# First convolution tap on ScalarE, and the first weights in another layout and queue

## The chip, the cores and the metric

The kernel runs on one core of a Trainium2 chip. The metric is device time in microseconds (us), the median of several executions. The core's engines work side by side, each through its own list of instructions in a fixed order, with semaphores between them: TensorE (PE: matmuls, weight loads shown as PEld), VectorE (DVE), ScalarE (ACT), GpSimd (POOL) and SyncE (SP, which here only issues DMAs). DMAs are issued from SP, ACT or POOL.

## The reference

One layer of a streaming encoder, on x of 1024 rows (the sequence) by 1024 columns, float32:

```python
h = x @ w_in + b_in                     # -> [xa | za | xb | zb | ga | gb], 1024 columns each
xa = causal_depthwise_conv(xa, conv_w, conv_b)          # 4 taps along the sequence
ya = rg_lru(xa, w_r, b_r, w_i, b_i, lam) * silu(za)     # branch A: gates, then a linear scan
yb = multiscale_pool(xb, w_pool, b_pool, scale) * silu(zb)   # branch B: windows 2, 4, 8, 16
merged = sigmoid(ga) * (ya @ w_proj_a) + sigmoid(gb) * (yb @ w_proj_b)
y = merged @ w_out + b_out
out = layer_norm(alpha * x + y, ln_gain, ln_bias)
```

The convolution of branch A is `y[t] = sum over k = 0..3 of x[t - 3 + k] * w[k], plus b`, per channel.

## The kernel before

All matmuls are in a split form: every float32 operand is split into a high part (a copy into the rounded type `F32R`, by ACT: `A.copy`) and a low part (raw minus high, by DVE), and a product is three passes: high x high, high x low, low x high (`passes`). On top of that the big products are done in blocks of halves with Strassen's scheme: seven products where eight would be, from sums of operands. The steps named m1 to m7 in class `Group` are these seven.

The feature axis is cut into blocks of 128 columns of h. A group takes two such blocks: `G` groups make gate columns (ga or gb), `A` groups the pair xa, za, and `B` groups the pair xb, zb. The list `order` runs G0, then A0, G1, A1, G2 and so on, then the B groups. After the groups come the two projections (`pa`, `pb`), and the product with `w_out` with the norm and the stores.

The first group, G0, has a path of its own, because nothing has been loaded yet: it is done without the seven products, as four quarters of x (`q`) times halves of the contraction (`kh`) and of the sequence (`h`), for both of its blocks (`n` = 0 and 1, blocks 32 and 36 of `w_in`). Its matmuls are called `ps_s` in the profile. Their weights lie in `wr[n]` (raw, `w0r` in the profile), `wh[n]` (high, `w0h`) and `wl[n]` (low, `w0l`). `dma_w0(n, a, b, h)` loads the parts a to b (of four, 128 rows of the contraction each) of block n, for one or both halves `h`; `split_w0` splits them. `dma_x(q, i, sl)` loads a piece of `xr[q][i]`, which holds two halves of x's quarter q; `split_x` splits it into `x13` (kh = h), `x2` and `xb` in the profile `x` and `xb`. For quarter 0 this goes piece by piece, in this order:

```python
    split_w0(0, 0, 1, slice(0, 1))
    for kh, h in ((0, 0), (1, 1), (0, 1), (1, 0)):
        if kh == h == 1:
            split_w0(0, 0, 1, slice(1, 2))
        for sl in PARTS if kh == h == 0 else (slice(0, H),):
            split_x(0, kh, h, sl)
            mm0(0, kh, h, 0, sl)
        if kh == h == 1:
            split_w0(1, 0, 1)
            mm0(0, 0, 0, 1)
        if kh or h:
            mm0(0, kh, h, 1)
```

So PE begins with the first block (n = 0) on two pieces of 256 columns of the half (0, 0), goes on with the first block on the half (1, 1), then the second block (n = 1) on (0, 0), the second block on (1, 1), and both blocks on (0, 1) (tile `xb`) and (1, 0) (tile `x`). `sum57` (the 128x1024 subtraction `t<-xr,xr` on DVE) prepares the sums of x for the groups that follow.

The order on each engine is not the order of the code. Every operation is recorded in a class `Plan`, which keeps PE's order as written and sorts the operations of the others by due times that follow from PE's order, on a clock of estimated costs (`cost`); `emit` then issues them in that order. All instructions therefore have one line number in the profile (L388, in `emit`). `within(us)` sets how long before or after its place in the code an operation is due: `within(-2 * SOON)` is four microseconds ahead, and puts DMAs early in their queue. The planner's costs know a DVE `tensor_scalar` into `xc` and an ACT `activation` with Identity as different prices, so that a moved operation can change the order of others.

`a_front(c, xp, zt)` is the convolution of an A group: from `xp` (the block's xa with three zero columns ahead) it makes `xc` by four taps over 128x1024, then splits `xc` into `xch` and `xcl`; `a_gates` multiplies those with the gate weights (matmuls `ps_g`), and goes on with sigmoid, exp, tanh, sqrt on ACT and the scan on DVE. There are eight A groups.

Of the kernel before, what the change touches and what calls it, by code (L numbers as in the profile page):

```python
# [11 lines left out]
F32 = mybir.dt.float32  # L12
F32R = mybir.dt.float32r
AF = mybir.ActivationFunctionType
ALU = mybir.AluOpType

P = 128
S = 1024
D = 1024
NK = D // P  # L20
# [24 lines left out]
C_CONVB = 48  # L45
C_CONVW = 56
# [354 lines left out]
def layer_kernel(ctx: ExitStack, tc: tile.TileContext, xq, x, w_in, par, wg, w_pool, wpa, wpb, w_out, rows, out):  # L401
    nc = Plan(tc)
# [18 lines left out]
    def wt(name, dt=F32R, shape=(P, 2, H)):  # L421
        return wpool.tile(list(shape), dt, tag="w", name=name)
# [4 lines left out]
    def kt(name, dt=F32, w=S):  # L427
        return kpool.tile([P, w], dt, tag="k", name=name)

    def et(name):  # L430
        return epool.tile([P, H], F32, tag="e", name=name)
# [9 lines left out]
    V, A = nc.vector, nc.scalar  # L441
# [4 lines left out]
    def pcol(base, c):  # L446
        return par_sb[:, base + c:base + c + 1]


    def split(raw, hi, lo):  # L450
        A.copy(hi, raw)
        V.tensor_tensor(lo, raw, hi.bitcast(F32), ALU.subtract)
# [147 lines left out]
    def blocks_of(kind, c):  # L600
        if kind == "A":
            return XA + c, ZA + c
        if kind == "B":
            return XB + c, ZB + c
        sec = GA if c < 4 else GB
        return sec + c % 4, sec + c % 4 + 4
# [141 lines left out]

    def a_front(c, xp, zt):
        xc = kt(f"xc{c}")  # L750
        V.tensor_scalar(xc, xp[:, 0:S], pcol(C_CONVW, 4 * c), pcol(C_CONVB, c), ALU.mult, ALU.add)
        for j in range(1, 4):
            V.scalar_tensor_tensor(xc, xp[:, j:j + S], pcol(C_CONVW, 4 * c + j), xc, ALU.mult, ALU.add)
        xh, xl = kt(f"xch{c}", F32R), kt(f"xcl{c}", F32R)
        split(xc, xh, xl)
        A.activation(zt, zt, AF.Silu, bias=pcol(C_BIN + ZA, c), scale=-1.0)
        return xc, xh, xl
# [146 lines left out]
    def b_pool(g):  # L904
# [15 lines left out]
        if g == 1:  # L920
# [5 lines left out]
    sp, m, nl, y, z, z2, acc = (const.tile([P, 8], F32, name=n)  # L926
                                for n in ("sp", "sp_m", "sp_nl", "sp_y", "sp_z", "sp_z2", "sp_acc"))
# [29 lines left out]
    for i in range(WARM):  # L957
        nc.tensor.matmul(psw, warm[:, 0:P], warm, start=True, stop=True)
    first = blocks_of(*order[0])
    wr, wh, wl = [[f(f"{t}{n}") for n in range(2)] for t, f in  # L960
                  (("w0r", lambda n: wt(n, F32)), ("w0h", wt), ("w0l", wt))]
# [6 lines left out]
    def w0_part(t, n, a, b):  # L968
        return t[n].rearrange("p h (k m) -> p h k m", m=P)[:, :, a:b, :]

    def dma_w0(n, a, b, h=slice(0, 2)):

        (A if a == 0 else nc.sync).dma_start(w0_part(wr, n, a, b)[:, h], w_in[first[n]].rearrange("p (h k) m -> p h k m", h=2)[:, h, a:b, :])

    def split_w0(n, a, b, h=slice(0, 2)):
        split(*(w0_part(t, n, a, b)[:, h] for t in (wr, wh, wl)))

    def dma_x(q, i, sl=slice(0, S)):
        nc.sync.dma_start(xr[q][i][:, sl], xq[q, i][:, sl])
# [21 lines left out]

    PARTS = [slice(0, H // 2), slice(H // 2, H)]
    dma_w0(0, 0, 1, slice(0, 1))
    with nc.within(-2 * SOON):
        for sl in PARTS:
            dma_x(0, 0, sl)
    dma_w0(0, 0, 1, slice(1, 2))
    dma_w0(1, 0, 1)
    dma_x(0, 0, HALF[1])
    dma_x(0, 1, HALF[0])  # L1010
    dma_x(0, 1, HALF[1])
# [65 lines left out]
    def each(f, qs, *a):  # L1077
        for q in qs:
            f(q, *a)

    split_w0(0, 0, 1, slice(0, 1))
    for kh, h in ((0, 0), (1, 1), (0, 1), (1, 0)):
        if kh == h == 1:
            split_w0(0, 0, 1, slice(1, 2))
# [8 lines that stand above are left out]
# [74 lines left out]
    for i in range(1, len(order)):  # L1167
        kind, c = order[i]
# [54 lines left out]
        if kind == "A":  # L1223
            def prev_end(c=c, tiles=tiles, i=i):
                front = a_front(c, *tiles)
                due.setdefault(i + 2, []).append(lambda: a_gates(c, *front, tiles[1]))
        elif kind == "B":
            def prev_end(c=c, tiles=tiles, i=i):
                for _ in b_front(c, *tiles):
                    pass  # L1230
                if c % 2 == 1:
                    pools.setdefault(i + 2, []).append(lambda: b_pool(c // 2))
        else:
            prev_end = finish
# [122 lines left out]
    for i, (n, j) in enumerate(steps):  # L1357
# [7 lines left out]
        if j == 1:  # L1365
            a, c, m1, um = [[None] * KQ for _ in range(4)]
        X_, W_ = ([(hi_[:, k, :], lo_[:, k, :]) for hi_, lo_ in ops[i][o:o + 2] for k in range(2)] for o in (0, 2))
        for g in range(KQ):
# [17 lines left out]
            if (n, j) in DONE:  # L1386
                d, h = DONE[n, j]
                d += g
                if j == 3:
                    t, u = ps, et(f"c12_{n}{g}") if n == "b" else None  # L1390
                else:
                    t = u = m1[g] if j == 2 else um[g][:, HALF[h]]
# [12 lines left out]
            if (n, j, g) in CASTS:  # L1405
                k = CASTS.index((n, j, g))
# [89 lines left out]
    a, c = ([None] * KQ for _ in range(2))  # L1496
# [89 lines left out]
```

## Time and profile before

| what | before |
|---|---|
| median of 3 runs | 742.84 us (742.25, 742.84, 745.42) |
| profiled execution, its own time | 743.09 us |
| its span | 741.3 us |
| PE busy, share of the span | 732.1 us, 99% |
| DVE busy | 599.6 us, 81% |
| ACT busy | 459.0 us, 62% |
| POOL busy | 68.2 us, 9% |
| moved by DMA | 158.98 MB, mean 214 GB/s |

The span runs from the first to the last instruction in the trace; the execution's own time has some 1.8 us around it. A row of a timeline or of the chain gives start, duration, engine, operation, written tile, read tiles, and in brackets how long the engine had stood idle ahead of it and for what. A row of waits gives the waiting instruction, whom it waited for, the sum, the number of times and the longest. A row of windows gives the stretch, its length, and each engine's busy time in it with the number of instructions (PE, PEld, DVE, ACT, POOL), then the granted clock, the DMA share and GB/s. A row of a tile gives durations in ns as least, median and largest.

### The profile page before, as it was taken

The numbers are of one execution on the slowest core, as the hardware profiler recorded it, in microseconds if no ns is written. First come the engines' busy times: TensorE is split into PE (matmuls) and PEld (weight loads), VectorE is DVE, ScalarE is ACT, GpSimd is POOL, SyncE is SP. The second block draws the span as 40 slices with busy tenths as digits, with TensorE's granted clock in tenths as the row PEclk, the third lists the DMA queues.
The fourth block names the chain that finished last, engine by engine and source line by source line (L and its number), as shares of the span: only waits on it lengthen the run. The fifth ranks groups of instructions, "written<-read, shape, count | busy, mean of one in ns | idle before, by whom it ended". The sixth has DMA issues, their size and how long they took to land.

```text
span 741.3 us, 8792 instructions
## 1 busy us (share of the span) xinstructions
PE 732.1 (99%) x3249; PEld 599.0 (81%) x3249; DVE 599.6 (81%) x749; ACT 459.0 (62%) x587; POOL 68.2 (9%) x118
## 2 busy tenths in 40 slices
PE   8999999999999999999999999999999999999996
PEld 6887887888788878888888888888888888888885
DVE  7999796959696878977986767879948886999676
ACT  7686959686877868688844445446543555324473
POOL 0071011111101111100011000100000000000021
PEclk9999999999999999999999999999999999999999
DMA  8237988588988989842187944998679996758657
GB/s 328 96 137 194 273 190 259 139 243 217 307 166 214 321 214 281 213 115 99 45 200 155 213 113 157 277 336 319 229 248 298 317 330 230 261 206 233 179 88 139
DMA packets 64227, 158.98 MB, mean 214 GB/s; under 512 B 4340, under 2 KB 8308, under 8 KB 64120
## 3 DMA queue, kind: packets, MB, share of 16 engines
q1 hardware_dynamic: 43512, 106.26, 41.3%
q0 software_dynamic: 20112, 51.91, 33.6%
q8 instruction: 25, 0.41, 0.2%
q10 hardware_dynamic: 560, 0.26, 0.1%
q14 instruction: 18, 0.15, 0.1%
HBM read 137.43 MB, written 77.07 MB: 289 GB/s over the span
## 4 chain that ended last, share of the span: by engine, by line
PE 98%; DMA 1%; DVE 1%; DVEq 0%; issue 0%
PE a_A L388 11%; PE a_B L388 11%; PE a_G L388 11%; PE oa L388 6%; PE pa_a L388 6%; PE pa_b L388 6%; PE c_B L388 6%; PE c_A L388 6%; PE c_G L388 5%; PE ps_pool L388 3%; PE oc L388 3%; PE pc_b L388 3%; PE pc_a L388 3%; PE e_B L388 3%; PE e_A L388 3%; PE ps_s L388 3%
## 5 line engine op out<-in xcount | busy, mean ns | idle before, releaser
L388 ACT ACT_TABLE_LOAD x38 | 48.8, 1283 | 3.0 <-issue 2.3
L388 DVE TENSOR_TENSOR i<-i,xc 128x1024 f32<-128x1024 f32 x8 | 9.8, 1224 | 26.6 <-ACT i L388 26.6
L388 DVE SCALAR_TENSOR_TENSOR xc<-xp,par_sb,xc 128x1024 f32<-128x1024 f32 x24 | 30.7, 1279 | 0.3
L388 PE MATMUL pa_a<-oh,oh 128*128 128x512 f32 x64 | 24.9, 389 | 0.0
L388 PE MATMUL pa_a<-oh,ol 128*128 128x512 f32 x64 | 24.9, 389 | 0.0
L388 PE MATMUL pa_b<-oh,oh 128*128 128x512 f32 x64 | 24.9, 389 | 0.0
L388 PE MATMUL pa_b<-ol,oh 128*128 128x512 f32 x64 | 24.9, 389 | 0.0
L388 PE MATMUL pa_b<-oh,ol 128*128 128x512 f32 x64 | 24.9, 389 | 0.0
L388 PE MATMUL pa_a<-ol,oh 128*128 128x512 f32 x64 | 24.9, 389 | 0.0
L388 ACT ACTIVATE zb<-zb,par_sb 128x1024 f32<-128x1024 f32 (+1 forms) x16 | 15.0, 939 | 13.7 <-DVE zb L388 13.6
L388 ACT ACTIVATE r<-ps_g,par_sb 64x512 f32<-64x512 f32 x32 | 21.9, 684 | 2.1 <-PE ps_g L388 1.2
L388 ACT ACTIVATE i<-ps_g,par_sb 64x512 f32<-64x512 f32 x32 | 21.9, 685 | 1.9 <-DVE r L388 1.4
L388 PE MATMUL c_A<-x64h,wd_A 128*128 128x512 f32 x64 | 21.0, 389 | 0.0
L388 PE MATMUL c_B<-x64h,wd_B 128*128 128x512 f32 x64 | 21.0, 389 | 0.0
L388 PE MATMUL ps_pool<-mixh,wp 128*128 128x512 f32 x64 | 20.6, 393 | 0.0
L388 POOL DMA_DIRECT2D out<-y x7 | 8.5, 1210 | 132.1 <-ACT sd L388 118.7
L388 PE MATMUL e_A<-x,wah_A 128*128 128x512 f32 x64 | 19.7, 389 | 0.0
L388 PE MATMUL e_B<-x,wah_B 128*128 128x512 f32 x64 | 19.7, 389 | 0.0
L388 POOL COPY paced<-pace 128x1 f32<-128x1 f32 x17 | 6.6, 387 | 128.7 <-ACT pace L388 128.7
L388 PE MATMUL c_G<-x64h,wd_G 128*128 128x512 f32 x56 | 18.4, 389 | 0.0
L388 DVE TENSOR_TENSOR_SCAN r<-a,i 128x1024 f32<-128x1024 f32 x8 | 18.3, 2282 | 0.1
L388 PE MATMUL e_G<-x,wah_G 128*128 128x512 f32 x56 | 17.2, 389 | 0.0
(521 smaller groups left out, 2535.9 us busy)
## 6 DMA issues: line engine op xcount, KB each, us to landing
sg<-sg SPq DMA_DIRECT2D x16, 512.0 KB, 3.6
ra_A<-in_w_in SPq DMA_DIRECT2D x8, 512.0 KB, 7.2
rb_A<-in_w_in SPq DMA_DIRECT2D x8, 512.0 KB, 7.8
xb<-bias SPq DMA_DIRECT2D x4, 1024.0 KB, 15.9
ya<-r SPq DMA_DIRECT2D x8, 512.0 KB, 6.3
xb<-in_x POOLq DMA_DIRECT2D x4, 1024.0 KB, 9.3
ra_B<-in_w_in SPq DMA_DIRECT2D x8, 512.0 KB, 4.8
rb_B<-in_w_in SPq DMA_DIRECT2D x8, 512.0 KB, 6.2
```

Source lines behind the costliest of these rows:

```text
L388: getattr(getattr(nc, t.op[0]), t.op[1])(*a, **k)
```

## The change

Three things are changed.

- In `a_front` the first tap, `xp[:, 0:S] * w[0] + b`, is an ACT activation (Identity with a scale and a bias per partition) instead of a DVE `tensor_scalar`. The three other taps stay on DVE.
- The first group's two weight blocks are laid out in DRAM quarter by quarter (first index the quarter, then the half), so that a quarter of both halves is one contiguous run per partition; the raw tile in SBUF has the same layout, and `split_w0` reads it through `w0_raw`. The high and low tiles keep their layout. The layout is made on the host before the launch.
- The second block's first quarter is issued from SP's queue instead of ACT's. It and the second piece of the first block's first quarter now stand inside `within(-2 * SOON)`. The very first high part (128x128) is made by DVE instead of ACT.

```diff
     def a_front(c, xp, zt):
         xc = kt(f"xc{c}")
-        V.tensor_scalar(xc, xp[:, 0:S], pcol(C_CONVW, 4 * c), pcol(C_CONVB, c), ALU.mult, ALU.add)
+        A.activation(xc, xp[:, 0:S], AF.Identity, bias=pcol(C_CONVB, c), scale=pcol(C_CONVW, 4 * c))
...
+    def w0_raw(n, a, b):
+        t = wr[n].rearrange("p a b -> p (a b)").rearrange("p (k h m) -> p h k m", h=2, m=P)
+        return t[:, :, a:b, :]
+
     def dma_w0(n, a, b, h=slice(0, 2)):
-        (A if a == 0 else nc.sync).dma_start(w0_part(wr, n, a, b)[:, h], w_in[first[n]].rearrange("p (h k) m -> p h k m", h=2)[:, h, a:b, :])
-
-    def split_w0(n, a, b, h=slice(0, 2)):
-        split(*(w0_part(t, n, a, b)[:, h] for t in (wr, wh, wl)))
+        lo_, hi_ = 2 * P * a + P * h.start, 2 * P * (b - 1) + P * h.stop
+        (A if n == a == 0 else nc.sync).dma_start(wr[n].rearrange("p a b -> p (a b)")[:, lo_:hi_],
+                                                  w_in[first[n]].rearrange("p k m -> p (k m)")[:, lo_:hi_])
+
+    def split_w0(n, a, b, h=slice(0, 2), high=A.copy):
+        raw, u, v = w0_raw(n, a, b)[:, h], w0_part(wh, n, a, b)[:, h], w0_part(wl, n, a, b)[:, h]
+        high(u, raw)
+        V.tensor_tensor(v, raw, u.bitcast(F32), ALU.subtract)
...
     with nc.within(-2 * SOON):
         for sl in PARTS:
             dma_x(0, 0, sl)
-    dma_w0(0, 0, 1, slice(1, 2))
-    dma_w0(1, 0, 1)
+        dma_w0(0, 0, 1, slice(1, 2))
+        dma_w0(1, 0, 1)
     dma_x(0, 0, HALF[1])
...
-    split_w0(0, 0, 1, slice(0, 1))
+    split_w0(0, 0, 1, slice(0, 1), V.tensor_copy)
...
+    w0 = blocks(w_in[0])
+    for n in (32, 36):
+        w0[n] = w0[n].reshape(P, 2, 4, P).transpose(0, 2, 1, 3).reshape(P, NK, P)
...
-        "w_in": blocks(w_in[0]),
+        "w_in": w0,
```

## The prediction

> **What bounds the kernel now.** I read the page first: the span, the busy shares, and the chain of work that ended last. Then the waits of TensorE (PE), and the windows.
>
> ```profile
> span 741.3 us, 8792 instructions
> PE 732.1 (99%) x3249; PEld 599.0 (81%) x3249; DVE 599.6 (81%) x749; ACT 459.0 (62%) x587; POOL 68.2 (9%) x118
> PE 98%; DMA 1%; DVE 1%; DVEq 0%; issue 0%
> PE ps_warm L388 <- DVE xp L388: 1.4, 1, 1.4
> PE ps_s L388 <- DVE xb L388: 0.3, 1, 0.3
> 9.95:731.12 721.17, 721.17 (x3205) 591.28 (x3206) 588.77 (x726) 452.07 (x574) 66.28 (x97) 1.00 0.75 215
> ```
>
> The chain is PE for 98% of the span. In the windows row the stretch from 9.95 to 731.12 us holds 721.17 us of PE work in 721.17 us: the matmuls follow each other without one gap. DVE (VectorE) is busy for 588.77 us of it and ACT (ScalarE) for 452.07 us, both under cover of PE. So shorter DVE or ACT work there is worth nothing, and only two places can give time: the 9.95 us ahead and the 10.2 us behind. The tail (norm and store of the last rows) is not touched. What is left is the start, row by row, with PE first.
>
> ```profile
> 4.42 0.58 PE L388 MATMUL ps_s<-x13h,w0h 128*128 128x256 f32 x1
> ...
> 5.07 0.41 PE L388 MATMUL ps_s<-x13h,w0l 128*128 128x256 f32 x1
> 5.28 0.41 PE L388 MATMUL ps_s<-x13h,w0h 128*128 128x256 f32 x1
> ...
> 6.47 0.79 PE L388 MATMUL ps_s<-x13l,w0h 128*128 128x512 f32 x1
> 7.07 0.59 PE L388 MATMUL ps_s<-x13h,w0l 128*128 128x512 f32 x1
> 7.75 0.50 PE L388 MATMUL ps_s<-x13h,w0h 128*128 128x512 f32 x1
> 8.09 0.40 PE L388 MATMUL ps_s<-x13l,w0h 128*128 128x512 f32 x1
> 8.33 0.40 PE L388 MATMUL ps_s<-x13h,w0l 128*128 128x512 f32 x1
> ...
> 9.27 0.39 PE L388 MATMUL ps_s<-xb,w0h 128*128 128x512 f32 x1
> 9.95 0.50 PE L388 MATMUL ps_s<-xb,w0h 128*128 128x512 f32 x1 [0.30 <-DVE xb L388]
> 10.29 0.40 PE L388 MATMUL ps_s<-xb,w0l 128*128 128x512 f32 x1
> ```
>
> The first column is the start. Two holes show: 7.07 to 7.75, and 9.27 to 9.95, where the pitch at full rate is 0.24 (8.09 to 8.33). Another thing shows: a matmul of 256 columns takes 0.21 us of pitch at 5.07, nearly as much as one of 512 at 8.09, so PE runs at about half rate until some time between 7.07 and 8.09, though the clock column below reads 1.00 there.
>
> What the holes wait for stands in the rows of the other engines:
>
> ```profile
> 0.73 1.34 SPq L388 DMA_DIRECT2D xr<-in_xq  x3
> 3.77 0.41 ACT L388 CAST x13h<-xr 128x256 fp32r<-128x256 f32 x1 [0.17 <-DMA xr<-in_xq]
> 4.08 0.29 ACT L388 CAST w0h<-w0r 128x128 fp32r<-128x128 f32 x1
> 5.08 0.62 ACT L388 CAST x13h<-xr 128x512 fp32r<-128x512 f32 x1 [0.17 <-DMA xr<-in_xq]
> 7.30 0.40 ACT L388 CAST w0h<-w0r 128x256 fp32r<-128x256 f32 x1 [1.60 <-DMA w0r<-in_w_in]
> 4.21 0.43 DVE L388 TENSOR_TENSOR x13l<-xr,x13h 128x256 fp32r<-128x256 f32 x1 [2.80 <-ACT x13h L388]
> 5.73 0.69 DVE L388 TENSOR_TENSOR x13l<-xr,x13h 128x512 fp32r<-128x512 f32 x1 [0.36 <-ACT x13h L388]
> 7.74 0.42 DVE L388 TENSOR_TENSOR w0l<-w0r,w0h 128x256 fp32r<-128x256 f32 x1 [1.31 <-ACT w0h L388]
> 8.08 1.22 DVE L388 TENSOR_TENSOR t<-xr,xr 128x1024 f32<-128x1024 f32 x1
> 9.21 0.69 DVE L388 TENSOR_TENSOR xb<-xr,xb 128x512 fp32r<-128x512 f32 x1
> ```
>
> Both holes have one origin. The 128x256 cast at 7.30 is the high part of the second block's first quarter (`split_w0(1, 0, 1)`); ACT sat idle 1.60 us until its DMA landed. PE's matmul at 7.75 reads it. The same cast held DVE for 1.31 us; then DVE goes w0l, the 1.22 us difference `t`, and the low part of `xb` from 9.21 to 9.90, for which PE stands until 9.95.
>
> **Part 1: the second block's first quarter goes to SyncE's (SP's) queue, third in it.** By its due time (`within(-2 * SOON)`) it is issued behind the two quarter-width pieces of x and ahead of the other half of `xr[0][0]`. Three issues took 1.34 us, 0.45 each, so the half and all later loads of SP are issued 0.45 us later, and ACT issues two instead of three. Whether the half lands later depends on the bytes:
>
> ```profile
> 1.45:3.70 2.25, 2.25 (x5) 1.81 (x6) 0.00 (x0) 1.28 (x1) 0.00 (x0) 1.00 0.76 213
> 3.70:4.42 0.72, 0.67 (x2) 0.00 (x0) 0.21 (x1) 0.65 (x3) 0.00 (x0) 1.00 0.76 260
> 4.42:5.92 1.50, 1.50 (x7) 1.50 (x7) 1.14 (x5) 1.10 (x3) 0.00 (x0) 1.00 0.96 333
> 5.92:7.75 1.83, 1.74 (x4) 0.62 (x3) 0.52 (x2) 0.45 (x2) 0.00 (x0) 1.00 1.03 390
> ```
>
> The last three columns are the granted clock, the DMA share and GB/s. Summed: 0.48 MB by 3.70, 0.67 by 4.42, 1.17 by 5.92, 1.88 by 7.75. From 4.42 on the engines are full, so the order of the bytes decides. After the change, two x pieces (131 KB each), the second block's quarter (131 KB) and the first block's two pieces on ACT's queue (65 KB each) are 0.52 MB: moved by about 3.9 us. With the x half (262 KB) it is 0.79 MB: 4.8 us. Before, its cast began at 5.08 after a 0.17 us wait, which is the same place, because the quarter competed with it from the other queue anyway. I take no delay for the half; the bound on the bad side is one issue, 0.45 us. The quarter lands at 4 to 5 us instead of 7.3. The next x half follows at 1.05 MB (5.6), the fourth at 1.31 MB (6.3), ahead of their casts.
>
> Then the 7.30 cast goes ahead of or behind the 5.08 one; DVE takes x13l at 5.73 to 6.42, w0l to 6.8, `t` to 7.9, xb's low part to 8.6. PE: 7.07 stays, the next matmul follows at half-rate pitch (2 x 0.21 = 0.43 us), then eight more at 0.24, so the third xb matmul starts at 7.07 + 0.43 + 1.92 = 9.42 instead of 10.29: **-0.87 us**. xb's low part is wanted at 9.2 and there at 8.6. From then on PE and DVE both run about a microsecond earlier, and DVE has the 1.3 us that it stood idle, so the later order keeps its margins.
>
> **Part 2: the layout.** `w_in`'s blocks 32 and 36 are reordered on the host so that a quarter of both halves is one run per partition: 1 KB where there were two of 512 B, 2 KB for the last two quarters. Same bytes, fewer packets. No row separates packets of that size; between 333 and 390 GB/s, 1.05 MB takes 3.1 or 2.7 us, so 0 to -0.45 us of transfer, nearly all of it behind 10 us where nothing waits. I take 0. The splits read the raw tile in another order, with the same inner run of 128: 0.
>
> **Part 3: the first high part on DVE.** ACT loses the 0.29 us cast at 4.08; DVE, idle 2.80 us until 4.21, gains a copy of that size. ACT's second x piece can start 0.2 us earlier, the first matmul at 4.2 (end of the 3.77 cast) instead of 4.42. But the next ones need DVE's low parts, one after the other, and DVE now has one more. Bounds -0.24 and +0.28; 0 taken, as the later DVE rows decide.
>
> **Part 4: the first tap on ScalarE.**
>
> ```profile
> L388 DVE TENSOR_SCALAR xc<-xp,par_sb x8: 804/806/809, 56.7 to 319.8; 128x1024 f32<-128x1024 f32 x8
> L388 ACT ACTIVATE z<-z,par_sb x8: 1152/1154/1159, 62.0 to 305.7; 128x1024 f32<-128x1024 f32 x8
> ACT xch L388 <- DVE xc L388: 12.5, 8, 2.5
> 67.48 1.22 DVE L388 TENSOR_TENSOR xcl<-xc,xch 128x1024 fp32r<-128x1024 f32 x1
> 72.60 1.58 PE ps_g L388 x12
> 75.00:100.00 25.00, 25.00 (x112) 20.67 (x111) 20.28 (x23) 22.36 (x28) 1.90 (x3) 1.00 0.95 275
> ```
>
> Removed: 8 x 0.806 = 6.4 us of DVE. Added: 8 ACT activations of 128x1024 with bias; the nearest row is 1.15 us, so 9.2 us of ACT, whose own range is the cast of that size (1.05) to 1.16. Both lie under PE's unbroken 721 us, in its first half. ACT's fullest 25 us there hold 22.36; with one tap, 23.5. Covered again, so 0. The cover: the tap makes DVE's three other taps wait for ACT once more. In the first A group (the tightest I found) xcl ends at 68.7 and PE reads it in the gate matmuls at 72.60: 3.9 us to spare. The tap adds 1.15 - 0.81 = 0.34 us and one hand-over of some tenths. ACT is in order: while the tap waits for xp, the casts and PSUM copies behind it wait too. Now `xch` makes ACT stand so for 12.5 / 8 = 1.6 us each time, 2.5 at most, and PE does not notice. A gain is excluded: nothing on PE waits for DVE here.
>
> **Sum.** -0.87 + 0 + 0 + 0. The profiled execution took 743.09 us, 1.8 more than its span; it becomes 742.2. It stands 0.25 above the median of the three runs (742.84), so I put the median at 742.0.
>
> **Rivals.**
>
> *The hole moves, nothing is gained.* The x half does land one issue later: its cast goes from 5.08 to 5.53, the matmul of 6.47 to 6.92 and that of 7.07 to 7.52. If the order on DVE also keeps xb's low part behind `t`, the second hole stays, and the time is 742.8 to 743.3. For it: that cast already waits for its DMA. Against it: the bytes above, and that the second block's quarter no longer runs beside it on the other queue. [...]
>
> *The clock.* What is brought forward may fall into the half-rate stretch. In my sum one matmul does. If the full rate is tied to how PE was busy before and the shift makes it come later, by half of what it took here, say (1.45 to 7.07 at least, so 2.8 us), 12 matmuls take 0.43 instead of 0.24: +2.3, less the 0.87: 744.3. If only the three matmuls from 7.5 are caught, the gain shrinks by 0.6, to 742.6. For it: the half-rate pitch at 5.07. Against it: the warm-up matmuls that PE runs from 1.45 are not touched. [...]
>
> *ScalarE becomes the bound (slower).* Place: the eight a_front calls between 56 and 325 us. If the tap is placed ahead of its input and holds ACT for more than the 3.9 us to spare, PE stops at the gates. It decides from 3.9 us of blocking on; at 5 us it is 1.1 us in each of 8 groups, +8.8, about 751; at 4.2 us +2.4, about 744.4. For it: ACT is at 22.36 of 25 us in one stretch, and the whole order is planned anew from costs. Against it: the longest such wait now is 2.5 us.
>
> **How the numbers follow.** Gain at the start as in the sum, or nearly (741.5 to 742.6): 0.60. Nothing gained: 0.23. Clock misses its moment: 0.05. ACT bound: 0.08, half of it over 746.6. More gained than the bounds (0.87 + 0.24 + 0.17 for the step from 6.47 to 7.07, which is 0.60 and not 0.43; so below 741.5): 0.04. The forecast is the first, 742.0. The range reaches down to 741.0 (that best case, with some room, as the three runs differ by 0.6 between the lower two) and up to 743.7 (no gain, one issue lost, the same room); the clock and the ACT case are left out above it. What a measurement of this kernel tells from no change is about 0.5%, 3.7 us. Since the whole start can give about 1.3 us by these rows, faster by more than that has 0.02; slower by more, half of the ACT case and a little, 0.05; the rest is within.
>
> **What would show it.** Right: the cast of `w0h` at 128x256 begins before 6 us without a wait for its DMA; PE has no hole at 7.07 or 9.27, and its third xb matmul stands at 9.3 to 9.6; from there to the last 256-wide matmuls the PE share is full, and that stretch is still 721 us long; DVE's busy time falls by 6.4 and ACT's rises by about 9. Wrong: the x half's cast waits until 5.5 or later (first rival); pitch 0.43 beyond 8 us (second); any wait of PE for xch, xcl or an ACT copy between 56 and 330 us (third). If the stretch from the start of the packed work to the end is longer than 721 us without such a wait, my view that PE's cover is complete is wrong.

## The result, and the profile after

| what | before | after |
|---|---|---|
| median | 742.86 us (742.24 to 745.42) | 744.8 us (743.15 to 747.08) |
| ratio, 95% interval | | 1.0028 [1.0022, 1.0034] |
| profiled execution, its own time | 743.09 us | 744.0 us |
| its span | 741.3 us | 742.2 us |
| PE busy | 732.1 us | 733.0 us |
| DVE busy | 599.6 us | 593.9 us |
| ACT busy | 459.0 us | 467.2 us |

The change costs 1.9 us, a quarter of a per cent. The forecast was a gain of 0.8 us: the sign was wrong, and the time lies above the range. The profiled execution of after stands 0.8 us below the median of after, so its trace shows 0.9 of the 1.9 us directly; the rest is taken up under the experiments.

I looked for the place first. The waits of PE (waiting instruction, whom it waited for, sum, times, longest), after:

```profile
PE ps_warm L388 <- DVE xp L388: 1.4, 1, 1.4
PE ps_s L388 <- ACT x13h L388: 0.3, 1, 0.3
```

and the window that answers to 9.95:731.12 of before, with the row of the new tap from the tile's view:

```profile
10.76:731.93 721.17, 721.17 (x3206) 591.15 (x3205) 581.65 (x716) 460.03 (x582) 66.43 (x97) 1.00 0.75 215
```

```profile
L388 ACT ACTIVATE xc<-xp,par_sb x8: 1245/1248/1260, 55.0 to 320.6; 128x1024 f32<-128x1024 f32 x8
```

The packed stretch is as long as it was, 721.17 us without one gap; it only begins 0.81 us later. The tap is there, 1.25 us each, 8 times, and no wait of PE names `xch`, `xcl` or an ACT copy. So the loss, like the expected gain, lies in the first 11 us. PE there (start, duration, what):

```profile
4.69 0.55 PE L388 MATMUL ps_s<-x13h,w0h 128*128 128x256 f32 x1 [0.32 <-ACT x13h L388]
5.04 0.47 PE L388 MATMUL ps_s<-x13l,w0h 128*128 128x256 f32 x1
5.47 0.58 PE L388 MATMUL ps_s<-x13h,w0l 128*128 128x256 f32 x1
...
6.28 0.41 PE L388 MATMUL ps_s<-x13h,w0l 128*128 128x256 f32 x1
6.79 0.79 PE L388 MATMUL ps_s<-x13h,w0h 128*128 128x512 f32 x1
7.52 0.79 PE L388 MATMUL ps_s<-x13l,w0h 128*128 128x512 f32 x1
8.11 0.63 PE L388 MATMUL ps_s<-x13h,w0l 128*128 128x512 f32 x1
8.54 0.63 PE L388 MATMUL ps_s<-x13h,w0h 128*128 128x512 f32 x1
...
9.82 0.54 PE L388 MATMUL ps_s<-x13h,w0h 128*128 128x512 f32 x1
10.20 0.40 PE L388 MATMUL ps_s<-x13l,w0h 128*128 128x512 f32 x1
10.43 0.40 PE L388 MATMUL ps_s<-x13h,w0l 128*128 128x512 f32 x1
...
11.12 0.40 PE L388 MATMUL ps_s<-xb,w0l 128*128 128x512 f32 x1
```

Both old holes (7.07 to 7.75 and 9.27 to 9.95) are gone, as predicted. But the third `xb` matmul starts at 11.12: not 9.42 as worked out, and 0.83 after before's 10.29. Two things are new. The first matmuls are late: 4.69 for 4.42, the third 5.47 for 5.07. And the pitch (from one start to the next) is 0.43 us from 8.11 to 9.82 and only then falls to 0.24. The first record of the granted clock in the trace, where the full rate begins, stands at 10.12 us, in before's trace at 7.49: the half rate lasts 2.6 us longer, the last 2 of them over work that was ready. What PE read at 4.69 and 6.79 came from ACT and DVE:

```profile
3.61 0.94 ACT L388 CAST x13h<-xr 128x256 fp32r<-128x256 f32 x2 [0.68 <-DMA xr<-in_xq]
4.46 0.29 ACT L388 CAST w0h<-w0r 128x128 fp32r<-128x128 f32 x1
5.49 0.40 ACT L388 CAST w0h<-w0r 128x256 fp32r<-128x256 f32 x1 [0.73 <-DMA w0r<-in_w_in]
6.12 0.62 ACT L388 CAST x13h<-xr 128x512 fp32r<-128x512 f32 x1 [0.24 <-DMA xr<-in_xq]
```

```profile
4.32 0.23 DVE L388 CAST w0h<-w0r 128x128 fp32r<-128x128 f32 x1 [2.92 <-DMA w0r<-in_w_in]
4.46 0.75 DVE L388 TENSOR_TENSOR x13l<-xr,x13h 128x256 fp32r<-128x256 f32 x2
5.13 0.49 DVE L388 TENSOR_TENSOR w0l<-w0r,w0h 128x128 fp32r<-128x128 f32 x2
```

The second block's quarter is cast at 5.49 instead of 7.30: that move worked. The x half behind it on SP's queue is cast at 6.12 instead of 5.08. And DVE waits for the very first weights until 4.32, then makes both `x13l` before the first `w0l`, where before it alternated. The windows of after say why data came late (length, busy times; at the end the granted clock, the DMA share, GB/s), with the half microsecond from 3.5 of both kernels, before's in the second fence:

```profile
1.45:3.70 2.25, 2.25 (x5) 1.81 (x6) 0.00 (x0) 1.37 (x2) 0.00 (x0) 1.00 0.60 180
3.50:4.00 0.50, 0.50 (x3) 0.14 (x1) 0.00 (x0) 0.39 (x1) 0.00 (x0) 1.00 0.80 87
3.70:4.42 0.72, 0.67 (x2) 0.00 (x0) 0.10 (x1) 0.59 (x2) 0.00 (x0) 1.00 0.68 117
4.42:5.92 1.50, 1.23 (x4) 1.01 (x5) 1.20 (x5) 0.73 (x3) 0.00 (x0) 1.00 1.06 322
```

```profile
3.50:4.00 0.50, 0.50 (x3) 0.15 (x1) 0.00 (x0) 0.33 (x2) 0.00 (x0) 1.00 0.98 346
```

By 5.92 the DMA engines have moved 0.97 MB where before it was 1.17. The gap opens around 3.5 to 4.4, where they are 0.80 and 0.68 busy at 87 and 117 GB/s. In the trace's list of packets six of 1 KB take 0.45 to 0.76 us each there, others of the same size some 0.05. By the order of their starts (267th to 283rd, behind the 256 of the two x pieces) they belong to the second block's quarter. In before's trace no packet that starts between 2.2 and 7 us takes more than 0.4.

### The profile page after: what moved, and what is told of

Read it like the earlier page. It is cut to its first block, busy times and chain, and to the rows that moved or that the text cites. A ratio compares the mean times of both kernels' runs of the same rounds, so it can differ in the third digit from the quotient of the medians.

```text
span 742.2 us, 8796 instructions
## 1 busy us (share of the span) xinstructions
PE 733.0 (99%) x3249; PEld 600.1 (81%) x3249; DVE 593.9 (80%) x742; ACT 467.2 (63%) x594; POOL 68.3 (9%) x118
## 4 chain that ended last, share of the span: by engine, by line
PE 98%; DMA 1%; DVE 0%; SPq 0%; DVEq 0%; ACT 0%; issue 0%
PE a_A L388 11%; PE a_B L388 11%; PE a_G L388 10%; PE oa L388 6%; PE pa_a L388 6%; PE pa_b L388 6%; PE c_B L388 6%; PE c_A L388 6%; PE c_G L388 5%; PE ps_s L388 3%; PE ps_pool L388 3%; PE oc L388 3%; PE pc_b L388 3%; PE pc_a L388 3%; PE e_B L388 3%; PE e_A L388 3%
```

## The experiments

Two theories. *Data:* the x half and the first weights land late, and that is the loss. *Clock:* the small holes that late data make before 7 us keep PE's rate at half until 10 us, and that is the loss. Against both: the tap costs something after all. Where an experiment undoes or does a part alone, its base is named; a ratio is always to the kernel before, timed on the same chip.

**The tap alone** (base: before).

```diff
-        V.tensor_scalar(xc, xp[:, 0:S], pcol(C_CONVW, 4 * c), pcol(C_CONVB, c), ALU.mult, ALU.add)
+        A.activation(xc, xp[:, 0:S], AF.Identity, bias=pcol(C_CONVB, c), scale=pcol(C_CONVW, 4 * c))
```

> The kernel before with the first tap on ScalarE and nothing else. If the loss is all in the start (theory 1: the x half lands a microsecond later and the half-rate stretch of TensorE lasts longer): as before, 742.9 us within 0.5, PE packed from 10 us on. If the tap costs time on ScalarE (rival): 744 to 745, with a PE wait between 56 and 330 us.

742.66 us against 742.54 for before on the same chip, 1.0001 [0.9992, 1.001]. The tap costs nothing that shows; the interval leaves room for 0.7 us, but after's trace has no wait of PE for it.

**The start alone** (base: after, with the diff above reversed).

> The changed kernel with the first tap back on VectorE. If the loss is all in the start: as the changed kernel, 744.8 us within 0.6, full matmul rate from about 10 us on. If the tap costs it: 742.0 to 742.9.

744.46 us, 1.0019 [1.0008, 1.003]. The loss is in the start, as far as the intervals tell. Its executions fall into two groups, 742.8 to 743.0 and 744.5 to 745.3, and the profiled one is of the first, with an own time of 742.82. PE in it:

```profile
4.66 0.54 PE L388 MATMUL ps_s<-x13h,w0h 128*128 128x256 f32 x1 [0.29 <-ACT x13h L388]
...
5.67 0.28 PE L388 MATMUL ps_s<-x13h,w0h 128*128 128x256 f32 x1
5.79 0.28 PE L388 MATMUL ps_s<-x13l,w0h 128*128 128x256 f32 x1
...
6.89 0.50 PE L388 MATMUL ps_s<-x13h,w0h 128*128 128x512 f32 x1 [0.71 <-ACT x13h L388]
...
10.05 0.39 PE L388 MATMUL ps_s<-xb,w0l 128*128 128x512 f32 x1
```

Data as late as in after (first matmul 4.66, the x half's cast at 6.22), but the full rate is there from 5.67 on (pitch 0.12 for 256 columns; the clock's first record is at 5.06). The third `xb` matmul starts at 10.05, 1.07 earlier than in after and 0.24 earlier than in before. With late data and an early clock the start is a little ahead of before's; by these profiles the loss takes both.

**After once more**, unchanged, for the spread.

> The changed kernel itself once more, for a second profile. If the late landing of the x half (6.0 us instead of 4.9) belongs to the new order of the DMAs: the cast of that half again begins at 5.8 to 6.3 us. If it was an accident of that one execution (a slow stretch of DMA at 3.5 to 4.4 us): it begins at 5.0 to 5.4, while the time stays 744.8. The full rate comes at 10 us in both executions if its moment is fixed by the kernel; elsewhere if it varies by execution.

745.08 us, 1.0029 [1.0017, 1.004]; executions from 742.80 to 746.46. The same kernel can end at 742.8, so what differs is not in its instructions.

**Eight warm-up matmuls for six** (base: after).

```diff
-WARM = 6
+WARM = 8
```

> The changed kernel with eight warm-up matmuls instead of six, so that PE is busy until about 5.2 us and has no hole from 4.4 to 4.7; the first real matmul starts some 0.5 us later. If the moment of the full rate depends on how busy PE was in the time ahead of it: full rate again at 7 to 8 us and 0.5 to 1.8 us less than the changed kernel, 743.0 to 744.3. If the late data alone cost the time and the clock's moment is fixed or random: 744.8 to 745.3.

743.78 us, 1.0014 [1.0005, 1.0022]. The first hole is filled and the full rate comes at 5.35, but the edit changed the planner's clock too, and a new wait of PE appeared, up to 322.8 us:

```profile
PE a_G L388 <- ACT u_G L388: 1.0, 1, 1.0
```

So the start gave more than the median shows. For the clock theory, but not clean.

**The layout alone** (base: before; the layout and `w0_raw`, with the old queue and order).

> The kernel before with the new layout of the two blocks alone: queues, due times and the ACT cast as before. If the slow DMA packets at 3.7 to 4.4 us come with the second block's quarter third on SyncE's queue: none here, the x half's cast at about 5.1 us, and the second block's quarter lands a little earlier than 7.3, as it is half as many packets on ScalarE's queue; 742.0 to 742.8 us. If the layout makes them: first matmul at 4.7, the x half's cast at 6, 744 to 745.

742.62 us against 742.64, 1.0006 [0.9997, 1.0015]. In the profile the x half's cast is at 5.47 and the third `xb` matmul at 9.61, and the own time is 742.39; but five of its eleven executions took 743.8 to 744.4, where none of the 23 of before beside them took over 743.13. No gain in sum.

**The queue alone** (base: before; the `dma_w0` conditions and the two lines moved into `within`, in the old layout, first high part on ACT).

```diff
-        (A if a == 0 else nc.sync).dma_start(w0_part(wr, n, a, b)[:, h], ...)
+        (A if n == a == 0 else nc.sync).dma_start(w0_part(wr, n, a, b)[:, h], ...)
```

> The kernel before with the second block's first quarter on SyncE's queue, third in it, and the two pieces due earlier; layout old (runs of 512 B), first high part on ScalarE. If the queue and the place do the harm: the x half's cast at about 6 us, times of two kinds, 743 and 745, median 744 to 745. If the layout does it: 742.0 to 742.9.

742.77 us, 1.0004 [0.9996, 1.0013]. The start is 0.97 us ahead of before (third `xb` at 9.32), as I had worked out for the whole change. It is given back: PE loses 0.4 us between 17.3 and 18.1 us to a `w0l` of DVE,

```profile
17.06 1.29 DVE L388 TENSOR_TENSOR w0l<-w0r,w0h 128x512 fp32r<-128x512 f32 x2
```

and the own time is 742.57 for 743.09, half of the gain; in the medians nothing is left. My sum had said that the later order keeps its margins; in this kernel it does not.

**The x half ahead of the quarter** on SP's queue (base: after).

```diff
+        dma_x(0, 0, HALF[1])
         dma_w0(1, 0, 1)
-    dma_x(0, 0, HALF[1])
```

> The changed kernel with the second block's first quarter fourth on SyncE's queue, behind the other half of x instead of ahead of it. If that quarter ahead of the x half is what delays the half: its cast back at 5.1 to 5.5 us, and 742.3 to 743.3. If the early hole at 4.4 to 5.9 us (one more thing on VectorE, the first weight piece late) is what keeps the clock low, times of two kinds stay and the median is 743.5 to 745.

746.5 us, 1.0052 [1.0038, 1.0066], the slowest. The x half is on time now (cast at 4.89), the quarter late (6.80), and the half rate lasts until 10.7. On top, PE waits between 51 and 54 us for weights of the next group:

```profile
PE c_G L388 <- ACT wbh_G L388: 0.9, 1, 0.9
PE c_G L388 <- DVE wbl_G L388: 0.6, 1, 0.6
```

The x half's lateness alone is therefore not the cause: with an early half and a late quarter the half rate lasted as long (10.7 for 10.12).

**The first high part back on ACT** (base: after).

```diff
-    split_w0(0, 0, 1, slice(0, 1), V.tensor_copy)
+    split_w0(0, 0, 1, slice(0, 1))
```

> The changed kernel with the very first high part on ScalarE again. If the copy on VectorE makes the hole ahead of PE's third matmul (5.04 to 5.47): that hole is gone and the clock comes up early in more executions, median 743.2 to 744.3. If it is the late landing of the first weights and of the x half: 744.3 to 745.2, as the changed kernel.

744.68 us, 1.0024 [1.0013, 1.0035]; no help. The hole ahead of the third matmul is gone (5.27 for 5.47). The profiled execution is a long one, 746.0: the x half was cast only at 6.89, and the half rate lasted until 13.6. Of the profiled executions only that of the kernel with the x half ahead took longer (746.5, with its waits at 51 to 54 us); here PE has no gap behind the start, so the start makes the loss.

**Idle matmuls in the holes** (base: after; one more warm-up and two more into `ps_warm` ahead of the x half's matmuls). The first form lets the planner count them, the second plans them at no cost, so that every engine keeps after's order.

```diff
-WARM = 6
+WARM = 7
...
+        if kh == h == 0:
+            for _ in range(2):
+                nc.tensor.matmul(psw, warm[:, 0:P], warm, start=True, stop=True)
```

> The changed kernel with three idle matmuls more on TensorE, which read the warm-up tile and write a bank that nobody reads: one behind the warm-up (from 4.4 us), two between the 256-column matmuls and the x half (from 6.3 us, where PE stands in the changed kernel). The data arrive as late as in the changed kernel. If the two kinds of times come from the clock, which comes up late where PE had holes: the full rate comes before 7.5 us in nearly all executions, one kind of times, median 742.5 to 743.4. If the late data alone make the time: 744.8 or more, still of two kinds.

> The changed kernel with the three idle matmuls of the run fill, but planned at no cost, so that the orders of VectorE, ScalarE and SyncE are those of the changed kernel and the stall at 321 us of fill is not there. If the clock is the cause: one kind of times, median 742.0 to 742.7. If the late data are: 744.5 or more.

The first: 743.35 us against 742.81, 1.001 [1.0001, 1.0019], with a wait of 0.8 us up to 322.7 us as in the warm-up case. The second: 743.61 against 742.75, 1.0014 [1.0004, 1.0025]. In the second one's profile the x half's cast is at 6.19, as late as in after, the full rate is there from 7.11, and the third `xb` is at 9.99; own time 742.56. Work that computes nothing takes back 1.0 to 1.3 us of the loss (1.0014 and 1.0010 for 1.0028). After's interval begins at 1.0022; the first form's ends below it, the second's, up to 1.0025, overlaps it. So some of the loss was the clock's, and its share is not sharply measured. It is not all of the loss: I had expected one group of times, and four executions of the second still took 744.5 to 745.7.

**Another address, another shape** (base: after). In the first the second block's quarters are rotated by 2 KB in their DRAM rows; in the second each quarter of both blocks is one contiguous 128 KB. The loads' source slices, not shown, follow.

```diff
-        w0[n] = w0[n].reshape(P, 2, 4, P).transpose(0, 2, 1, 3).reshape(P, NK, P)
+        w0[n] = np.roll(w0[n].reshape(P, 2, 4, P).transpose(0, 2, 1, 3), 2 if n == 36 else 0, axis=1).reshape(P, NK, P)
...
+        w0[n] = w0[n].reshape(P, 2, 4, P).transpose(2, 0, 1, 3).reshape(P, NK, P)
```

> The changed kernel with the second block's quarters rotated by two within each 4 KB row in DRAM, so that its first quarter is read from the bytes 2048 to 3071 of a row instead of 0 to 1023; same sizes, stride, queues and order. If the slow packets at 3.7 to 4.4 us come of the addresses (the x pieces, the first block's and the second block's first quarters all read the same quarter of 4 KB rows): none of over 0.4 us there, the first weights land by 4.1, the x half's cast at 5.3 to 5.6, 742.6 to 743.5 us. If they come of the size of the runs or the load: as the changed kernel, 744.8.

> The changed kernel with the two blocks stored quarter by quarter in DRAM over all partitions, so that a quarter is 128 KB in one piece and not 128 runs of 1 KB at a stride of 4 KB; SBUF, queues and order as in the changed kernel. If the stride is what makes the slow packets: none over 0.4 us before 4.5 us, 742.4 to 743.5. If not: 744.8.

745.02 us, 1.0033 [1.0021, 1.0044], and 744.55 us, 1.0022 [1.0012, 1.0032]. In the first no packet of 1 KB is slow, but some of 2 KB, the size of the x half's, take up to 1.25 us from 4.1 us on (up to 1.07 in after), and the x half's cast is at 6.78. The second still has the cast at 6.08. So another address or run length of the quarter does not cure it. The second's profile shows something else, in windows of 3.4 us:

```profile
1.19:4.60 3.41, 2.93 (x6) 1.84 (x7) 0.57 (x4) 2.23 (x4) 0.06 (x2) 1.00 0.72 206
4.61:8.01 3.40, 2.40 (x9) 1.55 (x10) 2.63 (x7) 1.69 (x4) 0.00 (x0) 1.00 0.77 264
8.02:11.43 3.41, 3.41 (x9) 2.64 (x8) 2.68 (x5) 2.11 (x5) 0.00 (x0) 0.50 1.01 398
11.44:14.84 3.40, 3.40 (x16) 2.82 (x15) 3.40 (x7) 3.16 (x5) 0.00 (x0) 1.00 1.06 391
```

The trace's first record of the granted clock stands at 4.61 and reads 1.00; from 8.02 to 11.43 the clock reads 0.50, with 9 matmuls in that row for 16 in the next, and behind it 1.00 again. From 4.61 to 8.02 and from 8.02 to 11.43 it is 3.41 us each; below, a window is a stretch of that length.

**One idle matmul** ahead of the x half's matmuls, in the queue-only kernel, and in the layout-only kernel (there at no planned cost).

> The old layout with the second block's quarter on SyncE's queue (queue_only) and one idle matmul on TensorE at its hole from 5.6 to 6.2 us. If holes keep the clock low: no execution above 743.2, median 742.2 to 742.7, so at or a little under the kernel before. If the clock is as good there without it: as queue_only, 742.8.

> The kernel before with the new layout alone, and one idle matmul on TensorE in the hole behind the 256-column ones (planned at no cost). The run layout_only had two kinds of times, about 742.3 and 744. If the slow kind is the clock: all executions under 743.2, median 742.1 to 742.5, a little under the kernel before. If the hole that remains is enough to lose the clock: two kinds again, median 742.3 to 743.9.

742.90 us, 1.0007 [0.9998, 1.0016], and 742.64 us, 1.0005 [0.9996, 1.0014]. Neither beats before. No version tried does. The expectations, no execution above 743.2, failed: four of twelve executions of the first took 744.4 to 744.7, three of eleven of the second 744.5 to 744.9. The queue-only kernel without the idle matmul had none above 743.71. So filling this hole does not remove the upper group of times; both profiles are of executions below it, and what makes it in these two kernels stays open.

**One warm-up matmul for six, before's order kept** (base: before; its planned cost is that of six).

> The kernel before with one warm-up matmul instead of six, planned as if it were six; all other orders, and the times at which data land, as before. If idle time of PE ahead of its real work sets how long it runs at half rate: full rate one window later, 743.5 to 745.5 us, times of two kinds. If the warm-up does not matter: 742.6 within 0.4.

743.09 us against 742.75, 1.0008 [0.9999, 1.0017]. The half rate lasts until 9.4, in before until 7.49, yet:

```profile
9.22 0.46 PE L390 MATMUL ps_s<-x13l,w0h 128*128 128x512 f32 x1
9.52 0.40 PE L390 MATMUL ps_s<-x13h,w0l 128*128 128x512 f32 x1
...
10.22 0.39 PE L390 MATMUL ps_s<-xb,w0l 128*128 128x512 f32 x1
```

The third `xb` starts at 10.22, as in before (10.29). In the old order PE waited for data until 9.95 anyway, so in this profile the late clock cost nothing; in after, 2 us of the longer half rate lay over work that was ready. The times say the same less sharply: two of the eleven executions took 744.46 and 745.20, and one, unexplained, 4224.93.

**The quarter back on ACT's queue** (base: after; the old condition in `dma_w0`), and **both pieces of the first quarter inside `within`**, so that the first is issued first (bases: after, and the queue-only kernel).

```diff
-    dma_w0(0, 0, 1, slice(0, 1))
     with nc.within(-2 * SOON):
+        dma_w0(0, 0, 1, slice(0, 1))
```

> The changed kernel with the second block's first quarter back on ScalarE's queue, all else changed. If the layout and SyncE's queue together make the x half late: its cast at about 5.5 us as in layout_only, median 742.4 to 743.6. If the copy on VectorE and the due times do it: 744.3 to 745.

> The changed kernel with the first piece of the first block's first quarter also inside the early due time, so that it is issued ahead of the second one again. If that swap is what makes the first weights late and the early hole: first matmul at 4.1 to 4.3 us instead of 4.7, third at 4.9 to 5.1 instead of 5.5, full rate before 8.5 us in most executions, median 742.6 to 743.8. If the late x half (slow packets at 3.7 to 4.4) decides alone: first matmul early, but the x half's cast at 6 and median 744.3 to 745.

> The old layout with the second block's first quarter on SyncE's queue, and the first block's first piece issued ahead of its second. Data land as in queue_only or earlier (x half's cast by 5.5 us, no slow packets before 4.5). 742.2 to 742.8 us; if the start is worth anything with all data early, 0.2 to 0.5 under the kernel before.

The first, 745.36 us, 1.0032 [1.0019, 1.0045], laid open what I had not read. The wait that PE had for its first weights, with the casts of both pieces ahead of it:

```profile
5.01 0.29 ACT L388 CAST w0h<-w0r 128x128 fp32r<-128x128 f32 x1
6.07 0.23 DVE L388 CAST w0h<-w0r 128x128 fp32r<-128x128 f32 x1 [1.58 <-DMA w0r<-in_w_in]
6.45 0.55 PE L388 MATMUL ps_s<-x13h,w0h 128*128 128x256 f32 x1 [2.08 <-DVE w0h L388]
```

The second piece (ACT's cast) was there at 5.01; for the first (DVE's) the engine waited until 6.07. `within` makes what stands inside it due earlier than what stands outside. After the change the second piece of the first quarter is inside, the first is not, so ACT issues the second piece first; in this kernel the second block's quarter as well, and PE starts at 6.45. (A wait of 1.4 us for `u_G`, up to 324.6 us, adds to this profile's 745.93.) With the first piece first, after's first matmul is at 4.17, but the x half's cast stays at 6.19 and the half rate lasts to 11.0: 744.79 us, 1.0039 [1.0026, 1.0051]. The queue-only kernel with this order becomes slower, 743.96 us, 1.0016 [1.0007, 1.0025]: the x half's cast slips from 5.53 to 6.38, in the old layout too, and its profile has the half rate once more from 8.03 to 11.44 (granted clock 0.50).

**The profiles side by side.** Over all twenty profiled executions the own time minus the start of the third `xb` matmul is 732.6 to 732.9 us in thirteen; the seven others have a wait or a half-rate stretch behind it. So the start decides. For the clock I counted back from each trace's first record of it in stretches of 3.41 us, the length between the records of the contiguous quarter's profile. In the one that ends at the first record PE was busy for 3.12 us or more in nineteen of the twenty; the exception is the contiguous quarter's profile above, with 2.93 ahead of 4.61. In the windows before that it was busy for 3.07 or less in all twenty. After's windows, and then that of the tap-only kernel, which happens to lie at the same time:

```profile
3.30:6.71 3.41, 3.07 (x9) 1.82 (x7) 1.73 (x6) 2.00 (x5) 0.00 (x0) 1.00 0.98 266
6.71:10.12 3.41, 3.33 (x7) 2.40 (x8) 3.12 (x4) 1.83 (x5) 0.00 (x0) 1.00 0.96 357
```

```profile
3.31:6.72 3.41, 3.37 (x11) 2.20 (x10) 1.86 (x5) 2.04 (x6) 0.00 (x0) 1.00 0.98 332
```

With before's start PE idled 0.04 us in that window, and the first record stands at 6.72; after idled 0.34 us, 0.32 of it ahead of the first matmul, and its first record stands at 10.12. The nearest cases in other profiles are the start-only kernel with 3.12 us, where the first record (5.06) follows, and the second run of after with 3.07, where none does:

```profile
1.65:5.06 3.41, 3.12 (x8) 2.04 (x8) 0.77 (x3) 2.29 (x4) 0.00 (x0) 1.00 0.73 191
```

```profile
2.77:6.18 3.41, 3.07 (x9) 1.93 (x9) 1.52 (x6) 1.58 (x5) 0.00 (x0) 1.00 0.96 254
```

The two differ by 0.05 us of a busy time whose matmul ends are modelled, and the 2.93 lies on the wrong side: fuller windows stood ahead of the full rate, but neither a limit nor what sets the moment is shown. That this moment makes the two groups of times from one kernel is my guess. Start-only and after fit it best: the same start, data as late, the first record at 5.06 and 10.12, and the third `xb` matmul at 10.05 and 11.12. That all the late executions come of this is not shown: few were profiled, and in the profile of 746.0 the data landed later still (the x half's cast at 6.89).

## Why the prediction was wrong, point by point

- **Part 1, "I take no delay for the half".** This step failed. The cast came at 6.12, 1.04 us late, beyond my bad end of 0.45. The step added bytes and divided by before's rates, and the rate itself changed: 87 GB/s for 346 from 3.5 to 4.0. The other half of Part 1 held: the quarter is early (5.49), both holes are gone, `xb`'s low part is there before it is wanted.
- **Part 3, "0 taken".** The bounds were for moving a copy. What moved as well, by `within`, was the order of ACT's two issues and DVE's order behind them: +0.27 us at the first matmul and +0.40 at the third, the latter beyond my +0.28. With the issue order put right the first is at 4.17; with the copy back on ACT the third is at 5.27 for 5.47. The prediction did not read the issue order at all.
- **"-0.87" at PE's pitch.** This step failed too. The sum took the full rate from where before had it, near 7.5; in after it came at 10.12. Against my 9.42 after stands at 11.12, 1.70 later: by the start-only profile, with the same late data and an early clock (10.05), 0.63 of it is data and 1.07 clock. The split is rough: that profile had the full rate from 5.06, earlier than my sum.
- **Rivals.** *The hole moves* and *the clock* came together. I priced each alone (742.8 to 743.3, and 744.3) and gave them 0.23 and 0.05; the measured 744.8 is nearest to the second's price, and in the profiles it is brought on by late data, of which the first is a part. My reason against the clock rival, that the warm-up matmuls are not touched, overlooked the idling after them: 0.32 us ahead of after's first matmul. With two more of them the full rate came at 5.35 for 10.12.
- **Part 4, the tap.** Right: no cost that shows, by the tap-only kernel and the unbroken 721.17 us. Its size was 1.25 us for my 1.15, ACT rose by 8.2 and DVE fell by 5.7 (9 and 6.4 forecast). The ScalarE rival did not happen.
- **Part 2, the layout.** 0 taken and 742.62 against 742.64 measured. Alone it is neutral in the median; the five executions of 743.8 to 744.4 are not explained.
- **The queue.** Alone, no gain either (1.0004). The profiled start did gain 0.97 but lost 0.4 again at 17 us; the remaining half does not show in the median.

What stays open: why the DMA engines are slow at 3.5 to 4.4 us with this set of loads. Layout alone and queue alone have the x half's cast at 5.5 to 5.8; together, with the quarter ahead of it on SP's queue, it is 6.1 to 6.9, and with the queue and the other issue order, in the old layout, 6.4. Address and run length of the quarter did not cure it. Slow packets alone do not make the half late: the tap-only kernel, with before's loads, has some of 2 KB of up to 1.18 us from 4.35 us on, and its cast is at 5.08. I did not find the rule. Open too is what after's own executions of 745 to 747 us look like: none was profiled.

## What to carry to other kernels

At the start of a kernel, work that is brought forward may land in TensorE's half-rate stretch, which here lasted until 10.12 us for 7.49: sum it with the rate that PE will have, and count the idle tenths of a microsecond that the change puts into the start: 0.34 us in after's window for 0.04 in the tap-only kernel's, with the first record of the clock at 10.12 for 6.72. When a due time is changed for one of two sibling loads, read the order in which they will be issued, not that of the code. And do not take a landing time from bytes over a mean rate where several small loads start together: here 87 GB/s were moved for 346 from 3.5 to 4.0 us, and the x half came 1.04 us late.

## What the runs showed of the hardware

- In the 3.41 us ahead of a trace's first clock record PE was busy for 3.12 us or more in nineteen of twenty profiles (start-only 3.12, after 3.33, tap-only 3.37) and for 2.93 in one (the contiguous quarter); in the stretches of that length before it, for 3.07 at most. In two profiles the granted clock read 0.50 for 3.41 us: from 8.02 to 11.43 in the contiguous quarter's, and from 8.03 to 11.44 in the queue-only kernel's with the first piece first. PE was busy for 2.40 and 1.84 us in the 3.41 us ahead of that; with 2.39 and 2.41 behind the first record, in the start-only kernel and the one with eight warm-up matmuls, the clock stayed at 1.00. No limit is shown.
- In after the profile's clock column reads 1.00 from 6.71 to 10.12, where the pitch is half (0.43 us for 512 columns at 8.11 to 9.82): ahead of the trace's first record of the clock the rate was read from the pitch.
- Single DMA packets of 1 KB took 0.45 to 0.76 us at 3.7 to 3.9 us in after, and up to 1.25 us in another profile (the x half ahead), where others of that size took 0.05. With another address of the quarter none of 1 KB was slow, but some of 2 KB were.
